# Moving a four-byte constant ahead of the identity, and 32 bytes of padding with it

## The chip, the cores and the metric

The kernel runs on one core of one Trainium2 chip. The metric is the device time of one execution in microseconds. Before the change it is 815.84 us, the median of three runs (815.72 to 816.29).

## The reference, cut to what matters

One layer of a hybrid decoder trunk over 512 tokens and 1024 channels, in float32.

```python
u = rmsnorm(h, norm1_g)
a_glu, q, k, v, r, g_low, gate_a, gate_b = split_cols(u @ w_in)
c = a_glu[..., :1024] * sigmoid(a_glu[..., 1024:])
c = silu(layernorm(causal_dwconv(c, width=31)))          # conv branch
y_conv = c @ w_conv_out
o = gla_chunked(q, k, v, log_sigmoid(g_low @ w_gate_up + b_gate) / 16)   # 4 heads
y_gla = (rmsnorm(o) * silu(r)) @ w_gla_out
h = h + (sigmoid(gate_a) * y_conv + sigmoid(gate_b) * y_gla) @ w_o
z = causal_dwconv(rmsnorm(h, norm2_g) @ w_ffn_up, width=3)
h = h + (silu(z[..., :2816]) * z[..., 2816:]) @ w_ffn_down
out = rmsnorm(h, final_g)
```

The layer norm of the conv branch needs `1 / sqrt(var + EPS)`. The constant of this case is the `EPS` that the square root takes as its bias.

## The kernel before, in words

Nearly all of the work is matrix products. Each float32 operand is split into a high part that TensorE's one-pass float32 format (F32R) holds exactly and a low remainder, and a product is made of three matmuls that add into one PSUM bank: `mm3`, lines 554 (moving high by stationary low, for a tile of output channels), 555 (low by high) and 556 (high by high). A weight block of 128 x 1024 arrives by DMA in a tile `raw`. ScalarE makes its high part `whi` (lines 435 and 468), VectorE its low part `wlo` (lines 437 and 477). Some products, on pairs or quads of tiles, are done in seven block products in place of eight; the sums that these need (`xq`, `usq`, `hq`, `gainq`, `btmpq`, `sumsq`, `sums`) are made by VectorE and GpSimd and split in the same way. Their matmuls are 256 columns wide where they go by tiles of output channels, the plain ones 512.

In a product by tiles of channels (`col_tile`) the activations move and the weights are stationary; in a product by tiles of tokens (`row_half` and the seven products of `w_r`, `w_o` and `w_down`) the weights move and the activations are stationary. The profile names the moving operand first: `mm<-uh,wlo` moves `uh` through `wlo`.

The order of the work is fixed when the program is built. `order` lists the weight blocks as they are used, `load`, `refill` and `split_weight` keep the loads and splits a few blocks ahead of TensorE, and `fill` places pieces of the conv taps and of the sums behind each weight split, by a share that the list gives each piece. The first stage is written out by hand (`manual_schedule`). Nothing of this order depends on where a tile lies in SBUF.

Where a tile lies is set by the order in which pools are opened and tiles are asked for. `const`, `weights`, `acts`, `temps`, `heap` and `conv` (later `ffn`) lie one behind the other from the low end of SBUF; `edge`, `gla`, `r`, `late`, `conv_hi` and `residual` are placed from the high end downwards. Every tile takes a multiple of 32 bytes of each partition: `eps`, four bytes, has byte 4448, and the next tile begins at 4480. The function `trunk_layer` opens the constant pool with a tile that nobody uses, `PADS[0]` bytes long (line 162); `PADS[1]` does the same for `edge`, `PADS[2]` for the middle of `temps` (line 852).

Byte addresses within a partition in the built program of before; the last column is what the argument uses.

| tiles | pool | first byte | byte modulo 256 |
|---|---|---|---|
| `ident` | const | 1568 | 32 |
| `pp` | const | 2080 | 32 |
| `ones`, `mhalf` | const | 3904, 4416 | 64 |
| `eps` | const | 4448 | 96 |
| `shares`, `run64`, `keep` | const | 4480, 4992, 6016 | 128 |
| `gains` | const | 6144 | 0 |
| `raw`, `whi`, `wlo` | weights | from 6176 on | 32 |
| `uh`, `ul`, `sums` | acts | from 55328 on | 32 |
| `x`, `un`, `xq`, `oa`, `gainq`, some `kept` | temps | from 88096 on | 32 |
| `tmp`, `btmp`, `btmpq` | temps | from 107680 on | 160 |
| `h`, `hq`, and `yh`, `sh`, `ah` and their low parts | heap, ffn | from 124704 on | 32 |
| `c`, `usq` | conv, ffn | from 177952 on | 32 |
| `ch` | conv_hi | from 199680 on | 0 |
| `sumsq` | late | from 216064 on | 0 |
| `hres` | residual | from 211968 on | 0 |
| `gate_up`, `att`, `q`, `k`, `state` | gla | from 200704 on | 0 |

A matmul reads pieces of these tiles that begin a multiple of 512 bytes further on, so their bytes have the same remainder. `ch` and `c` are the high and the low part of the conv branch's normalized channels (line 1063): `ch` lies at the high end, `c` at the low end.

`eps` is written once, by GpSimd at line 649, and read once, by ScalarE's square root at line 1044.

Of the kernel before, what the change touches and what calls it, by code (L numbers as in the profile page):

```python
# [10 lines left out]
F32 = mybir.dt.float32  # L11
# [7 lines left out]
P = 128  # L19
# [35 lines left out]
WARM = (6, 1)  # L55
MID = 4
EARLY = 2
PADS = (416, 992, 768)
ET = mybir.EngineType
SEVEN = {"w_o": KT // 2, "w_down": FT // 2, "w_r": KT // 2}  # L60

# [40 lines left out]
def trunk_layer(ctx: ExitStack, tc: tile.TileContext, a: dict, out: bass.AP):  # L102
    nc = tc.nc

    def pool(name, bufs, space=None):
        kw = {"space": space} if space is not None else {}
        return ctx.enter_context(tc.tile_pool(name=name, bufs=bufs, **kw))
# [7 lines left out]
    cp = pool("const", 1)  # L115
# [13 lines left out]
    def nm(s):  # L129
        return f"{s}_{next(names)}"  # L130
# [30 lines left out]
    for i, part in enumerate((cp, edge)):  # L161
        part.tile([P, PADS[i] // 4], F32, name=nm("pad"))


    ident = cp.tile([P, P], F32, name="ident")
    make_identity(nc, ident)
    pp = cp.tile([P, PP_N], F32, name="pp")
    gate_up = gp.tile([P, HEADS * DK], F32R, name="gate_up")
    ones = cp.tile([P, P], F32, name="ones")
    mhalf = cp.tile([P, NT], F32, name="mhalf")  # L170
    eps = cp.tile([P, 1], F32, name="eps")
    shares = cp.tile([P, P], F32R, name="shares")
    run64 = cp.tile([P, T], BF16, name="run64")
    keep = cp.tile([P, P], U8, name="keep")
# [2 lines left out]
    def load_consts():  # L177
        tc.keep_in_program_order(nc.sync.dma_start(pp, a["pp"]))
        nc.gpsimd.memset(shares.bitcast(F32), -1.0 / D)
        nc.gpsimd.memset(run64, 1.0)  # L180
        nc.gpsimd.memset(run64[:, 0:T:64], 0.0)

        kf = tmp(P)
        nc.gpsimd.memset(kf, 1.0)
        nc.gpsimd.affine_select(
            kf, kf, pattern=[[1, P]], compare_op=ALU.is_ge, fill=0.0, base=0, channel_multiplier=-1
        )
        nc.gpsimd.tensor_copy(keep, kf)
        nc.gpsimd.memset(att, 0.0)
# [661 lines left out]
    start.__exit__(None, None, None)  # L851
    tp.tile([P, PADS[2] // 4], F32, name=nm("pad"))
    load_consts()
# [1205 lines left out]
```

## Time and profile before

| | us |
|---|---|
| median of three runs | 815.84 |
| the profiled execution | 815.9 |
| its span, first to last instruction | 814.2 |
| TensorE (PE) busy in it | 806.4 |
| VectorE (DVE) busy | 708.0 |
| ScalarE (ACT) busy | 494.9 |
| GpSimd (POOL) busy | 188.5 |

The profiled execution takes 1.7 us more than its span and stands 0.06 us from the median. The granted TensorE clock is 0.999 of full. A matmul's own duration overlaps the next one's, so the distance between the starts of two matmuls is what a matmul costs; both are used below.

### The profile page before, as it was taken

To read this page: it belongs to the slowest core of one execution; us is meant where nothing else is said; L and a number is where in the kernel's file an instruction comes from. 1 tells how busy PE (TensorE), PEld (TensorE's weight loads), DVE (VectorE), ACT (ScalarE), POOL (GpSimd) and SP (SyncE) were. 2 spreads that over 40 slices of the span, in tenths; PEclk is the share of its full clock that TensorE was granted. 3 is DMA by queue.
4 is the path that set the end of the run, shared out by engine and by line. 5 is a ranking of instruction groups with operands and counts; after the bars stand their busy time and mean duration, and the time that the engine had idled before them with its cause. 6 is when DMAs were issued, how large, how long until landed. Compare 5 with 4: busy or idle time off the path is not lost.

```text
span 814.2 us, 11423 instructions
## 1 busy us (share of the span) xinstructions
PE 806.4 (99%) x4185; PEld 689.9 (85%) x4185; DVE 708.0 (87%) x1120; ACT 494.9 (61%) x761; POOL 188.5 (23%) x166
## 2 busy tenths in 40 slices
PE   9999999999999999999999999999999999999997
PEld 7888888788888798989888898898889988899885
DVE  6779999998998898786679899979966999789996
ACT  6667788677556785593434655556445563466655
POOL 2025433332204222022001100320133310612010
PEclk9999999999999999999999999999999999999999
DMA  9488858745832443432458513146632446334662
GB/s 334 150 195 174 197 159 173 164 114 129 197 85 83 148 125 104 146 113 96 164 126 205 187 60 122 52 155 156 148 128 87 141 118 167 106 104 158 178 130 105
DMA packets 41385, 115.71 MB, mean 142 GB/s; under 512 B 7960, under 2 KB 13216, under 8 KB 41328
## 3 DMA queue, kind: packets, MB, share of 16 engines
q1 hardware_dynamic: 33968, 89.01, 32.0%
q0 software_dynamic: 7200, 25.69, 18.2%
q8 instruction: 33, 0.54, 0.3%
q14 instruction: 24, 0.20, 0.1%
q10 hardware_dynamic: 160, 0.27, 0.1%
HBM read 110.76 MB, written 3.15 MB: 140 GB/s over the span
## 4 chain that ended last, share of the span: by engine, by line
PE 84%; DVE 14%; issue 1%; ACT 1%; DVEq 0%; ACTq 0%
PE mm L554 20%; PE mm L555 20%; PE mm L556 20%; DVE c L916 5%; PE cv L555 4%; PE cv L554 4%; PE cv L556 4%; DVE aside L916 3%; PE ax L556 2%; PE ax L555 2%; PE ax L554 2%; PE mm L772 1%; PE ax L1232 1%; PE ax L1234 1%; DVE wlo L437 1%
## 5 line engine op out<-in xcount | busy, mean ns | idle before, releaser
L554 PE MATMUL mm<-uh,wlo 128*128 128x512 f32 (+1 forms) x532 | 193.8, 364 | 0.3 <-DVE wlo L477 0.3
L555 PE MATMUL mm<-ul,whi 128*128 128x512 f32 (+1 forms) x532 | 191.6, 360 | 0.0
L556 PE MATMUL mm<-uh,whi 128*128 128x512 f32 (+1 forms) x532 | 191.5, 360 | 0.0
L437 DVE TENSOR_TENSOR wlo<-raw,whi 128x1024 fp32r<-128x1024 f32 x82 | 97.8, 1198 | 29.6 <-ACT whi L435 25.9
L405 POOL TENSOR_TENSOR raw<-raw,raw 128x512 f32<-128x512 f32 x39 | 60.6, 1554 | 241.0 <-DVE wlo L437 134.3
L554 PEld LDWEIGHTS mm<-uh,wlo 128*128 128x128 f32 x532 | 100.5, 189 | 15.8 <-DVE wlo L477 0.7
L556 PEld LDWEIGHTS mm<-uh,whi 128*128 128x128 f32 x532 | 100.4, 189 | 15.4
L555 PEld LDWEIGHTS mm<-ul,whi 128*128 128x128 f32 x532 | 100.5, 189 | 14.7
L435 ACT CAST whi<-raw 128x1024 fp32r<-128x1024 f32 x82 | 78.9, 965 | 36.9 <-PE mm L556 15.1
L468 ACT CAST whi<-raw 128x1024 fp32r<-128x1024 f32 x80 | 83.5, 1047 | 27.5 <-PE mm L556 13.1
L477 DVE TENSOR_TENSOR wlo<-raw,whi 128x1024 fp32r<-128x1024 f32 x50 | 64.7, 1299 | 7.2 <-ACT whi L468 7.1
L435 ACT CAST whi<-kept 128x1024 fp32r<-128x1024 f32 (+1 forms) x40 | 40.1, 1008 | 33.7 <-DVE kept L381 17.5
L437 DVE TENSOR_TENSOR wlo<-kept,whi 128x1024 fp32r<-128x1024 f32 (+1 forms) x40 | 48.3, 1211 | 5.5 <-ACT whi L435 5.4
L916 DVE SCALAR_TENSOR_TENSOR aside<-cv,pp,aside 128x255 f32<-128x255 f32 (+6 forms) x112 | 52.0, 465 | 0.0
L916 DVE SCALAR_TENSOR_TENSOR c<-aside,btmp,c 128x247 f32<-128x247 f32 (+13 forms) x93 | 52.0, 565 | 0.0
L916 DVE SCALAR_TENSOR_TENSOR c<-cv,pp,c 128x247 f32<-128x247 f32 (+13 forms) x93 | 43.1, 463 | 1.4 <-ACT c L912 1.4
L470 ACT ACTIVATE wlo<-raw 128x1024 fp32r<-128x1024 f32 x28 | 29.4, 1059 | 19.1 <-PE mm L554 19.1
L1770 DVE SCALAR_TENSOR_TENSOR tmp<-mm,pp,tmp 128x511 f32<-128x511 f32 (+1 forms) x42 | 31.2, 742 | 3.5 <-ACT tmp L1767 3.5
L1388 ACT COPY tmp<-mm 128x256 f32<-128x256 f32 x38 | 14.0, 368 | 30.3 <-PE mm L556 29.7
L1541 DVE TENSOR_TENSOR hres<-hres,mm 128x512 f32<-128x512 f32 (+1 forms) x37 | 24.6, 674 | 4.3 <-PE mm L556 2.5
L1770 DVE SCALAR_TENSOR_TENSOR tmp<-tmp,pp,tmp 128x511 f32<-128x511 f32 (+1 forms) x32 | 27.8, 888 | 0.4
L555 PE MATMUL cv<-ul,whi 128*128 128x512 f32 (+1 forms) x72 | 25.6, 356 | 0.0
(517 smaller groups left out, 2087.8 us busy)
## 6 DMA issues: line engine op xcount, KB each, us to landing
raw<-in_w_up_dram SPq DMA_DIRECT2D x44, 512.0 KB, 3.3
raw<-in_w_glu_dram SPq DMA_DIRECT2D x16, 512.0 KB, 4.9
raw<-in_w_down_dram SPq DMA_DIRECT2D x16, 512.0 KB, 4.5
wlo<-in_w_glu_dram POOLq DMA_DIRECT2D x12, 512.0 KB, 7.1
kept<-in_w_down_dram POOLq DMA_DIRECT2D x9, 512.0 KB, 5.3
raw<-in_w_v_dram SPq DMA_DIRECT2D x8, 512.0 KB, 6.4
raw<-in_w_qk_dram SPq DMA_DIRECT2D x8, 512.0 KB, 6.1
raw<-in_w_gb_dram SPq DMA_DIRECT2D x8, 512.0 KB, 4.4
```

What stands on the lines that cost most here:

```text
L405: work = nc.gpsimd.tensor_tensor(out, x, y, ALU.add)
L435: nc.scalar.copy(hi, raw)
L437: two_low[:] = [nc.vector.tensor_tensor(lo, raw, hi.bitcast(F32), ALU.subtract)]
L468: nc.scalar.copy(hi, raw)
L470: pace[0] = nc.scalar.mul(lo, raw, -1.0)
L477: pace[0] = nc.vector.tensor_tensor(lo, raw, hi.bitcast(F32), ALU.subtract)
L554: nc.tensor.matmul(acc, ll, rh, start=first, stop=False, **kw)
L555: nc.tensor.matmul(acc, lh, rl, start=False, stop=False, **kw)
L556: nc.tensor.matmul(acc, lh, rh, start=False, stop=last, **kw)
L916: nc.vector.scalar_tensor_tensor(out[:, j:], x[:, : half_t - j], w, out[:, j:], ALU.mult, ALU.add)
L1541: done = nc.vector.tensor_tensor(hres[t, n][:, c], hres[t, n][:, c], acc[:, c], op)
L1770: nc.vector.scalar_tensor_tensor(z[:, s:], acc[:, : T - s], w[j], z[:, s:], ALU.mult, ALU.add)
```

## The change

The tile `eps` is asked for before `ident` and not after `mhalf`, and the unused tile ahead of both shrinks by 32 bytes, from 416 to 384. No instruction is added, removed or written in another order.

```diff
-PADS = (416, 992, 768)
+PADS = (384, 992, 768)
...
+    eps = cp.tile([P, 1], F32, name="eps")
     ident = cp.tile([P, P], F32, name="ident")
     make_identity(nc, ident)
     pp = cp.tile([P, PP_N], F32, name="pp")
     gate_up = gp.tile([P, HEADS * DK], F32R, name="gate_up")
     ones = cp.tile([P, P], F32, name="ones")
     mhalf = cp.tile([P, NT], F32, name="mhalf")
-    eps = cp.tile([P, 1], F32, name="eps")
     shares = cp.tile([P, P], F32R, name="shares")
```

## The prediction

> **What bounds the kernel now.** I read the page's busy times first, then TensorE's waits, then the chain that ended last.
>
> ```profile
> span 814.2 us, 11423 instructions
> PE 806.4 (99%) x4185; PEld 689.9 (85%) x4185; DVE 708.0 (87%) x1120; ACT 494.9 (61%) x761; POOL 188.5 (23%) x166
> PE 84%; DVE 14%; issue 1%; ACT 1%; DVEq 0%; ACTq 0%
> PE mm L675 <- DVE ones L647: 1.1, 1, 1.1
> PE mm L554 <- DVE wlo L477: 0.3, 1, 0.3
> ```
>
> TensorE is busy for 806.4 of 814.2 us and waits by name for 1.4 us in all, never for a DMA. So the time is the sum of the distances between matmul starts, and a change that moves only addresses matters through that distance first. I therefore asked whether it already differs with where the operands lie. The chain shows two stages with the same work, 512-column matmuls in groups of three; each row is a start and a length in us.
>
> ```profile
> 500.54 0.23 PE cv L556
> 501.22 0.23 PE cv L556
> 501.90 0.23 PE cv L556
> ...
> 404.87 0.23 PE mm L556
> 405.57 0.23 PE mm L556
> ...
> 425.87 0.23 PE mm L556
> ```
>
> In the first stage a group of three takes 0.68 us (501.22 - 500.54). In the second, 30 groups take 425.87 - 404.87 = 21.00 us, 0.70 each. The clock is granted in full in both. The second is the product by `w_conv`, with `ch` moving. The durations, by operands (line, operation, count: minimum/median/maximum ns, or busy us, mean ns):
>
> ```profile
> L554 PE MATMUL mm<-uh,wlo 128*128 128x512 f32 x384 | 151.8, 395 | 0.3 <-DVE wlo L477 0.3
> L555 PE MATMUL mm<-ul,whi 128*128 128x512 f32 x384 | 149.7, 390 | 0.0
> L556 PE MATMUL mm<-uh,whi 128*128 128x512 f32 x384 | 149.6, 390 | 0.0
> L556 PE MATMUL mm<-whi,yh 128*128 128x512 f32 x30 | 11.7, 389 | 0.0
> L554 PE MATMUL mm<-ch,wlo x48: 397/397/400, 364.8 to 425.9; 128*128 128x512 f32 x48
> L556 PE MATMUL mm<-ch,whi x48: 390/397/397, 365.2 to 426.4; 128*128 128x512 f32 x48
> L555 PE MATMUL mm<-c,whi 128*128 128x512 f32 x48 | 18.9, 393 | 0.0
> L554 PE MATMUL cv<-ch,wlo x16: 392/396/400, 376.1 to 403.5; 128*128 128x512 f32 x16
> L556 PE MATMUL mm<-whi,sumsq x12: 389/396/397, 268.5 to 279.0; 128*128 128x512 f32 x12
> L555 PE MATMUL mm<-wlo,sumsq x12: 393/396/397, 268.2 to 278.7; 128*128 128x512 f32 x12
> L554 PE MATMUL mm<-whi,sumsq x8: 393/395/397, 268.0 to 272.9; 128*128 128x512 f32 x8
> L555 PE MATMUL cv<-wlo,sumsq x4: 394/397/397, 273.8 to 275.9; 128*128 128x512 f32 x4
> ```
>
> Where both operands have remainder 32 modulo 256 (`uh`, `ul`, `yh`, `whi`, `wlo`), an undisturbed matmul has 389. Where one has 0 and the other 32, it has 395 to 397, whether the odd one moves (`ch`) or is stationary (`sumsq`). `c` has remainder 32 itself, but alternates with `ch`, and has 393. 397 + 393 + 397 against three times 389 is 20 ns, which is the 0.70 against 0.68 of the chain. Two more rows say whether it is the remainder itself or the difference between the two operands that counts. These are 256 columns wide.
>
> ```profile
> L556 PE MATMUL ax<-gainq,whi x32: 283/283/283, 536.6 to 751.9; 128*128 128x256 f32 x32
> L556 PE MATMUL mm<-btmpq,whi x28: 276/280/284, 554.9 to 750.4; 128*128 128x256 f32 x28
> L555 PE MATMUL cv<-sumsq,whi x12: 277/279/285, 294.0 to 343.8; 128*128 128x256 f32 x12
> L554 PE MATMUL mm<-sumsq,wlo x28: 280/282/364, 292.4 to 396.9; 128*128 128x256 f32 x28
> ```
>
> `gainq` (difference 0) sits at exactly 283, every time. `btmpq` has remainder 160, a difference of 128; `sumsq` 0, a difference of -32. Both scatter in the same band around 280, though one starts on a multiple of 64 bytes and the other doesn't. I read this as a fixed rhythm that matmul and weight load fall into when their bytes agree modulo 256, and that they miss otherwise: at 512 columns the rhythm is the faster state, at 256 the slower by 1 to 4 ns. An equal shift of both operands leaves it.
>
> The Trainium skill ("TensorE: Matmul & The Clock Gate", section Step-by-step) says that TensorE has two independent SBUF read ports, so that loading the next weights takes no read bandwidth from the running matmul. By that rule the operands' relative place can't matter, and the terms below would all be nothing. The 397 against 389 speaks against it here.
>
> **The change part by part.** The unused tile loses 32 bytes and `eps` takes them, so `ident`, `pp`, `ones` and `mhalf` stay. `shares` and all that follows from the low end begin 32 bytes lower. The high end stays. Remainders 32 become 0, 160 becomes 128, `shares` 96. No instruction, wait, DMA or queue position is added or moved: the write of `eps` and its one reader stay where they are in their queues.
>
> 1. *Pairs that both move* (nearly all matmuls): same difference, same rhythm, 0. No row shows a one-pass pair with 0 and 0. Its bounds are the odd rows: 8 ns more for 512 columns (397 against 389), 7 ns less for 256 columns (276 against 283). I take 0, by the evidence of `btmpq` and `sumsq`.
>
> 2. *`ch` by weights* changes to difference 0. There are 64 + 64 matmuls with `ch` (two forms of 48 and two of 16) and 64 with `c`, so 64 groups at 20 ns: -1.28 us. Some comes back, because the rhythm takes a few matmuls to find after a change of width:
>
> ```profile
> L554 PE MATMUL mm<-uh,wlo 128*128 128x512 f32 x4 | 1.6, 394 | 0.0
> L555 PE MATMUL mm<-ul,whi 128*128 128x512 f32 x3 | 1.2, 393 | 0.0
> ```
>
> These are the first ones after narrow matmuls, between 530 and 538 us: 4 x 5 + 3 x 4 = 32 ns for one start. The `ch` matmuls stand between narrow ones for their first half; I count some eight starts, 0.25 us, an estimate. Net -1.0, between 0 and -1.3.
>
> 3. *`sumsq` stationary*: 12 + 12 + 8 + 4 = 36 matmuls at 7 ns, -0.25. They end in the one stage in which the chain leaves TensorE for ScalarE and VectorE, and a part of it may be waited away: -0.15, between 0 and -0.25.
>
> 4. *`sumsq` moving*, 256 columns: it finds the slower rhythm. The rows give 1 ns (282 to 283) for the larger forms and 4 for the smaller, about 100 matmuls: +0.2, between 0 and +0.4.
>
> 5. *Other engines.* A copy and a subtraction of 128 x 512 with tiles at remainder 0, and with none:
>
> ```profile
> L1063 ACT CAST ch<-btmp x8: 602/614/622, 348.3 to 363.8; 128x512 fp32r<-128x512 f32 x8
> L1351 ACT CAST btmpq<-xq x2: 619/620/620, 480.0 to 482.1; 128x512 fp32r<-128x512 f32 x2
> L1064 DVE TENSOR_TENSOR c<-btmp,ch x8: 677/683/1774, 349.0 to 364.4; 128x512 fp32r<-128x512 f32 x8
> L1356 DVE TENSOR_TENSOR usq<-xq,btmpq x2: 684/684/685, 496.6 to 500.6; 128x512 fp32r<-128x512 f32 x2
> out_dram<-tmp SPq DMA_DIRECT2D x2, 256.0 KB, 2.6
> out_dram<-hres SPq DMA_DIRECT2D x2, 256.0 KB, 2.7
> ```
>
> 614 against 620 and 683 against 684 ns; a store from remainder 160 lands in 2.6 us, from 0 in 2.7. I take 0 for all of it. What hides a difference of a few per cent is that TensorE waits for them for 0.3 us; if that cover went, 1% of VectorE's 708 us would be 7 us.
>
> Sum: -1.0 - 0.15 + 0.2 = -0.95 us. The profiled execution is 815.9 us (814.2 of span and 1.7 around it), which becomes 814.95; the median of the runs shown, 815.84, becomes 814.9.
>
> **The rivals.** *The places don't matter* (the skill's two ports): then `ch` is slow for a reason of its own, such as lying at the high end, and the time stays at 815.84. For it: no row shows `ch` by weights with difference 0. Against it: `sumsq` as stationary operand shows the same 7 ns in another product at another time.
>
> *A start on a multiple of 256 is itself faster*, so that a matmul spares a piece of its reading. Price by the scattered rows, 7 ns (276 against 283): on the 3 x 384 matmuls with `uh` and `ul` alone -8 us, 807.8; with the others up to twice that. Against it: `sumsq` starts on such a multiple and is no faster than `btmpq`. The skill's page on TensorE (section Back-to-back issue gap) gives 512 / 2.4 + 2.5 = 216 ns as the distance for 512 columns; the chain's 0.68 / 3 is 227, so by that page there are 11 ns to win, some 13 us on these 1,152 matmuls.
>
> *Remainder 0 is itself slower*, for the moving operand as for the stationary one. The rows with `ch` and `sumsq` fit this too, since every slow one has a 0 in it. It decides at the first `uh` matmul: 389 becomes 397, and 3 x 384 x 8 ns is +9.2 us, 825.0, with the other wide groups up to 832. Against it: `btmpq` has no 0 in it and loses the rhythm all the same.
>
> *A VectorE instruction falls behind GpSimd's.* In the stage near 285 us one subtraction on the chain lasts nearly twice its mean:
>
> ```profile
> 285.59 2.23 DVE wlo L437
> L437 DVE TENSOR_TENSOR wlo<-raw,whi 128x1024 fp32r<-128x1024 f32 x82 | 97.8, 1198 | 29.6 <-ACT whi L435 25.9
> ```
>
> Shifted by 0.2 us, a second one could do so: +1.0 us, which with the sum gives 815.9.
>
> **How the numbers follow.** Forecast 0.60, no effect of places 0.12, faster starts 0.15, slower starts 0.08, the VectorE collision 0.05. About 0.2% (1.6 us) is what a measurement of this kernel can tell from no change; that is 814.2 below and 817.5 above. The forecast's bounds on terms 2 to 4 run from -1.55 to +0.4, and a little more where the rhythm is found more often than now; I give 0.18 of its 0.60 to more than 1.6 us. Faster: 0.15 + 0.18 = 0.33. Slower: 0.08 + 0.03 from a collision of two = 0.11, and 0.01 for what I have not seen. Same: 0.55. The range holds the forecast, no effect and the collision, with the small end of the faster starts: 812.2 to 816.8. It leaves out the large ends on both sides, some 0.2.
>
> **What would show it.** Right: the medians of `mm<-ch,wlo` and `mm<-ch,whi` go to 389, the groups in the `w_conv` stage stand 0.68 us apart, `sumsq` moving shows 283, and `uh` by `wlo` stays at 389 and 283. `ch` still at 397 means that the places don't matter. `uh` at 397, or below 385, means that the remainder itself counts, and makes the prediction wrong, as would a new wait of TensorE of over 2 us.

## The result and the profile after

The changed kernel takes 814.39 us, the median of 21 runs (813.86 to 815.13), against 815.84 us for the kernel before (815.32 to 816.29, 21 runs). The ratio is 0.9983, with a 95% interval of 0.9977 to 0.9989: 1.45 us less, and by the interval between 0.9 and 1.9 us. The forecast was 814.9 us, 0.95 us less. The larger part of the chance, 0.55, went to a change of less than 1.6 us either way, and that is how it came out, though a change of zero lies outside the interval.

The page and TensorE's waits after the change:

```profile
span 813.4 us, 11423 instructions
PE 805.4 (99%) x4185; PEld 690.3 (85%) x4185; DVE 707.8 (87%) x1120; ACT 494.8 (61%) x761; POOL 191.7 (24%) x166
PE mm L675 <- DVE ones L647: 1.1, 1, 1.1
PE cv L554 <- DVE r L1598: 0.3, 1, 0.3
PE cv L555 <- DVE wlo L437: 0.2, 1, 0.2
PE mm L779 <- DMA raw<-in_w_v_dram: 0.2, 1, 0.2
```

The instructions are the same, in the same order on every engine; TensorE's share of the span is the same and its named waits, 1.8 us in all, stay far below 1% of it. What changed is how long a few of its matmuls take. Groups of matmuls and single operands after the change, in the two forms used before (busy us, mean ns; or minimum/median/maximum ns):

```profile
L554 PE MATMUL mm<-uh,wlo 128*128 128x512 f32 x384 | 152.0, 396 | 0.0
L555 PE MATMUL mm<-ul,whi 128*128 128x512 f32 x384 | 149.8, 390 | 0.0
L556 PE MATMUL mm<-uh,whi 128*128 128x512 f32 x384 | 149.7, 390 | 0.0
L554 PE MATMUL mm<-ch,wlo x48: 388/390/397, 365.0 to 425.3; 128*128 128x512 f32 x48
L556 PE MATMUL mm<-ch,whi x48: 388/389/390, 365.5 to 425.8; 128*128 128x512 f32 x48
L555 PE MATMUL mm<-c,whi 128*128 128x512 f32 x48 | 18.7, 390 | 0.0
L556 PE MATMUL mm<-whi,sumsq x12: 388/389/390, 268.7 to 278.9; 128*128 128x512 f32 x12
...
L555 PE MATMUL mm<-wlo,sumsq x12: 389/389/390, 268.5 to 278.7; 128*128 128x512 f32 x12
L555 PE MATMUL cv<-sumsq,whi x12: 282/283/284, 294.1 to 344.1; 128*128 128x256 f32 x12
L556 PE MATMUL ax<-gainq,whi x32: 283/283/284, 535.9 to 751.1; 128*128 128x256 f32 x32
L556 PE MATMUL mm<-btmpq,whi x28: 276/280/285, 554.1 to 749.7; 128*128 128x256 f32 x28
```

`ch` went from 397 to 389 and 390, `c` between them from 393 to 390, `sumsq` as stationary operand from 396 to 389. `sumsq` as moving operand of 256 columns went up from 279 to 283. `uh` and `ul`, whose start and whose weights' start moved together, stayed within 1 ns, and `btmpq`, 128 bytes off its weights before and after, stayed at 280. In the `w_conv` stage the chain now has the distance of the undisturbed stages, 407.56 - 406.88 = 0.68 us for three:

```profile
406.88 0.23 PE mm L556
...
407.56 0.23 PE mm L556
```

Six points of the trace bound five stages; 6.2 to 6.3 us follow the start of the last matmul. The table has the distance between the starts of the first or last matmuls with the operand named, in us, from one profile of each kernel (the third is the changed kernel profiled again with the last experiments):

| from | to | before | after | again |
|---|---|---|---|---|
| start | first `sumsq` | 268.01 | 268.30 | 267.60 |
| first `sumsq` | first `oa` | 27.65 | 27.53 | 27.51 |
| first `oa` | first `ch` | 69.10 | 69.19 | 69.20 |
| first `ch` | last `ch` | 61.65 | 60.74 | 60.74 |
| last `ch` | last matmul | 381.49 | 381.43 | 381.51 |

The `ch` stage is 0.91 us shorter in both, the stage with `sumsq` stationary 0.12 to 0.14, and the stage from `oa` on, in which `sumsq` moves, 0.1 longer. From the first `sumsq` to the end of the span it is 546.18 us before, 545.12 after and 545.19 again. The first stage differs by 0.7 us between two profiles of one and the same kernel, and most of that (0.5 us) is there before 36 us.

### The profile page after: what moved, and what is told of

It reads as the page before. It is cut to its first block, busy times and chain, and to the rows that moved or that the text cites. A ratio compares the mean times of both kernels' runs of the same rounds, so it can differ in the third digit from the quotient of the medians.

```text
span 813.4 us, 11423 instructions
## 1 busy us (share of the span) xinstructions
PE 805.4 (99%) x4185; PEld 690.3 (85%) x4185; DVE 707.8 (87%) x1120; ACT 494.8 (61%) x761; POOL 191.7 (24%) x166
## 4 chain that ended last, share of the span: by engine, by line
PE 77%; DVE 14%; issue 5%; ACT 1%; DMA 1%; POOL 1%; SPq 0%; DVEq 0%; ACTq 0%; POOLq 0%
PE mm L554 18%; PE mm L555 18%; PE mm L556 18%; DVE c L916 5%; PE cv L555 4%; PE cv L556 4%; PE cv L554 4%; DVE aside L916 3%; PE ax L556 2%; PE ax L555 2%; PE ax L554 2%; PE mm L772 2%; DVE wlo L437 2%; DMA raw<-in_w_v_dram 1%; PE cv L772 1%
## 5 line engine op out<-in xcount | busy, mean ns | idle before, releaser
L555 PE MATMUL mm<-ul,whi 128*128 128x512 f32 (+1 forms) x532 | 191.7, 360 | 0.0
L405 POOL TENSOR_TENSOR raw<-raw,raw 128x512 f32<-128x512 f32 x39 | 63.7, 1633 | 239.4 <-DVE wlo L437 121.4
```

The source lines that it names most:

```text
L405: work = nc.gpsimd.tensor_tensor(out, x, y, ALU.add)
L555: nc.tensor.matmul(acc, lh, rl, start=False, stop=False, **kw)
```

## The experiments

**Is it the difference, or the start itself?** The kernel before, with the high end moved up instead of the low end down:

```diff
-PADS = (416, 992, 768)
+PADS = (416, 960, 768)
```

> The kernel before, with one change: the unused tile at the high end is 960 bytes, not 992, so that everything placed from the high end lies 32 bytes higher. ch, sumsq, hres, att have remainder 32 modulo 256, as uh and the weights have had all along: the difference between the two operands of a matmul is 0, but no start is a multiple of 256. Theory (the difference counts): the same gain as the change, some 1.4 us, 814.4 us; mm<-ch,wlo and mm<-ch,whi at 389 to 390 ns, sumsq moving at 283. Rival (a start on a multiple of 256, or of 64, is what counts): nothing of the gain, since every start now misses such a multiple: 815.8 us or more, ch at 396.

Measured: 815.02 us against 815.70 for the kernel before on the same chip, ratio 0.9993 (0.9984 to 1.0002). The time alone doesn't settle it, since its interval takes in no change and most of the change's gain. The rows do. The first two are `ch`, the third `sumsq`, the last one of TensorE's waits:

```profile
L554 PE MATMUL mm<-ch,wlo x48: 389/389/396, 364.1 to 424.3; 128*128 128x512 f32 x48
L556 PE MATMUL mm<-ch,whi x48: 389/389/389, 364.5 to 424.8; 128*128 128x512 f32 x48
L555 PE MATMUL cv<-sumsq,whi x12: 283/283/283, 293.2 to 343.1; 128*128 128x256 f32 x12
PE cv L554 <- DVE r L1598: 0.4, 1, 0.4
```

None of these operands starts on a multiple of 256, and `ch` has its 389 all the same; its stage takes 60.74 us, as after the change. For these rows the start itself is not what counts. The time, though, missed the forecast of 814.4 us by 0.6, and the kernel with the low end moved down by 32 bytes, on the same chip in the next experiment, had 814.43. Some of that can be seen. The matmuls with `sumsq` stationary are at 389 here too, but their stage takes 27.63 us: the next matmul waits for VectorE, and the distance to it from the last of them grew from 0.54 us to 0.80, after the change only to 0.69. From the first `sumsq` to the end it is 545.35 us, 0.8 less than before, where the change had 1.1. What else the low end gives is not shown.

**The shift without moving `eps`.**

```diff
-PADS = (416, 992, 768)
+PADS = (384, 992, 768)
```

> The kernel before, with the unused tile at 384 bytes and eps left behind mhalf: the shift of 32 bytes alone. ident, pp, ones and mhalf move with the rest here. Theory: all of the change's gain comes from the shift, so 814.4 us, and where eps and the identity lie is worth nothing. Rival: the constants' own place counts (eps and ident), then it stays away from 814.4 by 0.5 us or more.

Measured: 814.43 us, ratio 0.9986 (0.9977 to 0.9994), 1.27 us less than the kernel before. All of the gain that can be told is the 32 bytes; where `eps` and the identity lie is worth nothing that can be told.

**The dose: all weights off by 32 bytes.** A pad ahead of the weights and one behind them, so that only `raw`, `whi` and `wlo` move:

```diff
         part.tile([P, PADS[i] // 4], F32, name=nm("pad"))
+    wp.tile([P, 8], F32, name=nm("pad"))
+    up.tile([P, 56], F32, name=nm("pad"))
```

> The changed kernel with raw, whi and wlo 32 bytes higher (a pad of 32 bytes ahead of them, one of 224 behind), so that every matmul of the split products has a difference of 32 between its operands. Theory: some 2,590 matmuls of 512 columns lose 6 to 7 ns each and some 1,250 of 256 columns win about 2: +16 to +18 us less 2.5, about 828 us; mm<-uh,wlo goes from 389 to 395 to 397 wherever undisturbed. Rival (the high end of SBUF is slow for ch): uh stays at 389 and the time at 814.4 us.

Measured: 826.12 us, ratio 1.0128 (1.0114 to 1.0142), 11.7 us over the changed kernel's 814.4. The two added lines move the lines of `mm3` from 554 to 556 on, here and in some runs below.

```profile
span 824.6 us, 11423 instructions
...
L556 PE MATMUL mm<-uh,wlo 128*128 128x512 f32 x384 | 153.6, 400 | 0.0
L557 PE MATMUL mm<-ul,whi 128*128 128x512 f32 x384 | 151.8, 395 | 0.0
L558 PE MATMUL mm<-uh,whi 128*128 128x512 f32 x384 | 151.9, 396 | 0.0
L556 PE MATMUL mm<-uh,wlo 128*128 128x256 f32 x148 | 41.8, 282 | 0.0
```

`uh` and `ul` lie where the changed kernel has them, and lose 4 to 6 ns each because their weights moved. So `ch` isn't slow for lying at the high end. The expected 828 us was 2 us too high: the mean loss in these groups is 5 ns, not 6 to 7, because part of these matmuls were out of the rhythm before (the group means were 396 and 390, not 389). 2,590 x 5 ns less 1,250 x 1.5 ns is 11.1 us, an estimate. The `ch` stage, again with a difference of 32, went back to 61.60 us.

**A map of places.** 32 matmuls to a group, with the moving operand's start set off by a number of bytes:

```python
acc = ps.tile([P, T], F32, tag="mm", name=name, bufs=4)
for i in range(count):
    s = dw // size + P * (i % 8)
    o = d // size + (n * (i % 2) if n < T else 0)
    nc.tensor.matmul(acc[:, :n], ww[:, s : s + P], mm[:, o : o + n], start=i == 0, stop=i == count - 1)
```

> Nothing of the layer: a row of matmuls, 32 to a group, that take weights of 128 columns from one F32R tile and move 512 (wide) or 256 (half) columns of another. The group's name has the byte by which the moving operand's start differs from the weights' start modulo 256 (d0 to d240 in steps of 16), or the byte by which both are shifted (both16, both32, both64, both128); three groups in bfloat16 (bf). Theory: wide has its shortest distance, 227 ns, at d0 and at all four of both, and 233 at d32 and d224 (that is, -32); half has 120 at d0 and about 118 elsewhere. Rival (absolute start counts): both32 differs from d0. Open, without a forecast: how wide the good place is (16, 32, 64 bytes), and if some difference is better than 0.

Groups of the map (busy us of the group, mean ns of one):

```profile
L39 PE MATMUL wide_d0x<-m,w 128*128 128x512 f32 x32 | 7.4, 390 | 0.0
L39 PE MATMUL wide_both16x<-m,w 128*128 128x512 f32 x32 | 7.5, 392 | 0.0
L39 PE MATMUL wide_both64x<-m,w 128*128 128x512 f32 x32 | 7.4, 390 | 0.0
L39 PE MATMUL wide_d32x<-m,w 128*128 128x512 f32 x32 | 7.6, 396 | 0.0
L39 PE MATMUL wide_d224x<-m,w 128*128 128x512 f32 x32 | 7.6, 396 | 0.0
L39 PE MATMUL half_d0x<-m,w 128*128 128x256 f32 x32 | 4.0, 283 | 0.0
L39 PE MATMUL half_d64x<-m,w 128*128 128x256 f32 x32 | 3.8, 276 | 0.0
L39 PE MATMUL bf_d0x<-mb,wb 128*128 128x512 bf16 x32 | 7.1, 380 | 0.0
L39 PE MATMUL bf_d32x<-mb,wb 128*128 128x512 bf16 x32 | 7.1, 379 | 0.0
```

The mean distance from one start to the next, in ns, worked out from the starts in each group without its first eight:

| difference, bytes | 0 | 32 | 64 | 96 | 128 | 160 | 192 | 224 |
|---|---|---|---|---|---|---|---|---|
| 512 columns | 226.7 | 233.3 | 228.9 | 233.4 | 233.1 | 234.3 | 233.2 | 233.4 |
| 256 columns | 120.0 | 116.7 | 113.3 | 119.8 | 118.6 | 117.3 | 113.3 | 118.4 |

Of the steps of 32 bytes that tiles can take, 0 alone has the 226.7 at 512 columns. Both operands shifted by 32, 64 or 128 have it too (226.7 to 227.1). Shifted by 16, both together, they don't: 229.9 ns, against the forecast. So the difference alone is not the whole rule: an equal shift kept the rhythm at the multiples of 32 that were tried, which is all that a tile's place can be, and not at 16. The 256 columns are slowest at 0, with 96 hardly faster. The bfloat16 groups have 216 ns at all three of their places (0, 32 and 128); only F32R showed a dependence.

**A finer map, and narrower weights.** The same loop with steps of 4 bytes, and weights of 64 and 32 columns:

> Nothing of the layer: the same row of matmuls as the first map of places, 24 to a group, with the difference in steps of 4 bytes from 0 to 80 and from 224 to 252, and, in groups with w64 and w32 in the name, weights of 64 and 32 columns at differences of 0, 32 and 64 bytes. Theory (the load of the next weights meets the moving operand's reading): with narrower weights the slow places go, and 512 columns come down towards the 216 ns that bfloat16 had at every place; at full weights the good place around 0 and 240 is 16 to 20 bytes wide. Rival (the moving operand's own reading is slow at those places): the narrower weights change nothing at a difference of 32, 233 ns.

| difference, bytes | 0 | 4 | 12 | 20 | 28 | 60 | 64 | 236 | 240 | 244 | 252 |
|---|---|---|---|---|---|---|---|---|---|---|---|
| 512 columns | 226.7 | 236.6 | 228.9 | 240.0 | 226.7 | 226.7 | 228.9 | 226.7 | 226.7 | 240.0 | 226.7 |
| 256 columns | 120.0 | 123.4 | 116.7 | 123.5 | 118.3 | 116.7 | 117.8 | 116.6 | 117.5 | 122.9 | 120.0 |

There is no single good place 16 to 20 bytes wide: good and bad ones alternate every few bytes. At 64 bytes and 256 columns the two maps disagree, 113.3 against 117.8 ns, so the difference alone doesn't fix the rhythm; what ran just before was another group. The narrower weights went against the theory; the rival's forecast, no change at a difference of 32, nearly held (233.5 ns with 128 columns, 231.0 with 64, 232.2 with 32), but it had no place for a change at 0:

```profile
L39 PE MATMUL wide_w32d0x<-m,w 128*32 128x512 f32 x24 | 5.7, 394 | 0.0
L39 PE MATMUL wide_w32d32x<-m,w 128*32 128x512 f32 x24 | 5.7, 394 | 0.0
L39 PE MATMUL half_w32d0x<-m,w 128*32 128x256 f32 x24 | 2.9, 276 | 0.0
```

With 32 columns of weights the 512-column distance is 231.6 and 232.2 ns at differences of 0 and 32, and never comes near 216. That the next weights' load collides with the moving operand's reading is thus not shown. The width of the weights does change the distance at a difference of 0 (from 226.7 to 231.6, and from 120.0 to 113.3 at 256 columns), but a narrower product also has fewer rows of output, so this doesn't show that it is the load. What the rhythm is made of stays open.

**A better layout, first try.** Only tiles that move 256 columns at a time are laid off the weights by 64 bytes:

```diff
-PADS = (384, 992, 768)
+PADS = (384, 992, 640)
...
+    tp.tile([P, 16], F32, name=nm("pad"))
+    hp.tile([P, 16], F32, name=nm("pad"), bufs=1)
...
+    fp.tile([P, 16], F32, name=nm("pad"))
...
+            if not padded:
+                padded.append(fp.tile([P, 16], F32, name=nm("pad")))
...
+            late_pad.append(late.tile([P, 16], F32, name=nm("pad")))
...
+            chp.tile([P, 48], F32, name=nm("pad"), bufs=1)
```

> The changed kernel, with the tiles that move only 256 columns at a time laid 64 bytes off the weights (xq, gainq, btmpq, usq at a remainder of 64, sumsq at 192), by pads of 64 bytes and of 192; all others keep a remainder of 0. The map of places gives 113.3 ns at 64 and 192 for 256 columns, against 120 at 0 and 118 at 128; for 512 columns 229 at 64 against 227. Theory: 224 matmuls with xq and gainq, 96 with usq and 100 with sumsq win 6.7 ns, 64 with btmpq 4.7: -3.1 us; 96 with oa, which shares xq's slots, and 36 with sumsq stationary lose about 2: +0.3. Less 0.3 for hq, which stays at 0 between sumsq's matmuls: -2.5 us against the changed kernel, some 811.9 us, a ratio of 0.995. Rival (in the real order, in which the same weights are loaded twice, the places of the map don't hold): 814.4 us.

Measured: 814.55 us, ratio 0.9988 (0.9979 to 0.9997) to the kernel before, so nothing that can be told from the changed kernel.

```profile
L558 PE MATMUL ax<-xq,whi x32: 279/279/279, 530.1 to 745.0; 128*128 128x256 f32 x32
L557 PE MATMUL ax<-usq,whi x32: 279/279/279, 530.0 to 744.9; 128*128 128x256 f32 x32
L556 PE MATMUL mm<-oa,wlo x28: 388/394/481, 294.7 to 352.4; 128*128 128x512 f32 x28
L556 PE MATMUL mm<-whi,sumsq x8: 392/392/392, 267.2 to 272.0; 128*128 128x512 f32 x8
```

The 276 of the first map didn't come: `xq` and `usq` have a duration of 279, the value of the second map, in place of 283. What a matmul costs, the distance between starts, fell by less: `xq` by `whi` from 119.9 to 118.2 ns, not to 113.3. The last stage is 0.37 us shorter than after the change (381.06 against 381.43) and the `ch` stage, in which `sumsq` moves too, 0.15; the stage from `oa` on is 0.41 longer (69.60 against 69.19), mainly since `oa` went from 389 to 394. `sumsq` as stationary operand has 392 against 389. So what was won was given back.

**A better layout, second try.** By the finer map, a difference of 60 bytes costs nothing at 512 columns and wins 3 ns at 256. The activations of the up-projection move both widths, so their tiles get 256 spare bytes and they begin 15 elements in:

```diff
+    def act_tile(name, at=0):
+        t = up.tile([P, 4 * T + 64], F32R, tag="u", name=nm(name), bufs=4)
+        return t[:, at : at + 4 * T].rearrange("p (k t) -> p k t", k=4)
...
-            u2.extend(new_acts())
+            u2.extend(new_acts(15))
```

> The changed kernel itself, on the chip of the next two, to compare them with it: some 1.3 us below the kernel before, 814.3 us.

> The changed kernel with the second set of activations (uh and ul of the up-projection) 60 bytes further on in their tiles, so that 600 matmuls of 512 and 432 of 256 columns have a difference of 60 between moving operand and weights. The finer map gives 226.7 ns at 60 for 512 columns, as at 0, and 116.7 for 256, against 120 at 0. Theory (the map holds in the real order): uh by wlo at 512 columns stays at 389, at 256 goes from 283 to 279 or 280; 432 x 3.3 ns = -1.4 us, 812.9 us. Rival (which rhythm a stream falls into depends on more than the difference, as the two maps disagree at 64: 113.3 and 117.8): the 512-column matmuls lose the rhythm too, up to 600 x 6.7 ns = +4 us.

> The same, and xq, gainq, btmpq and usq with a remainder of 64, sumsq left at 0. Those four showed 279 to 280 ns at 64 in the run before, against 283, and 281 for btmpq: 320 x 3.5 and 64 x 1 ns = -1.2 us; 84 to 96 matmuls with oa showed 388 to 394 against 389: +0.3. Theory: -0.9 us more than with the activations alone, 812.0 us. Rival: what is won in TensorE is waited away elsewhere; then TensorE's waits grow.

Measured on one chip, against 815.66 us for the kernel before:

| kernel | us | ratio to before | 95% interval |
|---|---|---|---|
| the changed kernel | 814.27 | 0.9984 | 0.9975 to 0.9993 |
| activations 60 bytes off | 813.53 | 0.9973 | 0.9963 to 0.9983 |
| and four 256-column tiles 64 bytes off | 812.87 | 0.9965 | 0.9951 to 0.9979 |

The groups from 430 us on, after the change and with the activations 60 bytes off:

```profile
L556 PE MATMUL mm<-uh,whi 128*128 128x512 f32 x152 | 59.2, 389 | 0.0
L556 PE MATMUL mm<-uh,whi 128*128 128x256 f32 x88 | 24.9, 283 | 0.0
```

```profile
L556 PE MATMUL mm<-uh,whi 128*128 128x512 f32 x152 | 59.1, 389 | 0.0
L556 PE MATMUL mm<-uh,whi 128*128 128x256 f32 x88 | 24.4, 278 | 0.0
```

And with the four tiles as well, TensorE's longest wait and one of these tiles:

```profile
L557 PE MATMUL ax<-usq,whi 128*128 128x256 f32 x32 | 8.9, 278 | 0.0
...
PE mm L675 <- DVE ones L647: 1.1, 1, 1.1
```

The time fell by 0.74 us from the first row to the second, where 1.4 was forecast; the medians' intervals are too wide to tell the two apart. Durations would say 432 x 5 ns = 2 us, but they are not the cost. The stage in which these matmuls lie, from the last `ch` to the last matmul, says 1.14: 381.51 us in the changed kernel, 380.37 with the activations 60 bytes off. The profiled spans differ by 812.8 - 811.0 = 1.8 us, of which 0.65 is the first stage, which varies by that much. With the four tiles as well the last stage falls to 379.40, another 0.97, but the stage from `oa` on goes from 69.18 to 69.76, so 0.58 of it is lost again, twice what was forecast for `oa`. The third kernel is 2.8 us faster than the kernel before and 1.4 faster than the changed one; its interval and the changed kernel's overlap, but it is the lowest of all in the medians, and TensorE's longest wait stayed 1.1 us.

## Why the prediction was right

*What bounds the kernel.* That the change comes through the distance between matmul starts held from the first `sumsq` on. TensorE's named waits were 1.4 us before and 1.8 us after, of which 1.1 is the same one. Copies, subtractions and stores at the new places gave nothing that could be seen, as term 5 had it (the copy to `ch` 614 ns before and 618 after, the subtraction 683 and 682); GpSimd's busy time rose from 188.5 to 191.7 us, but no wait of TensorE names it.

*The reading of `btmpq` and `sumsq`* was the step that carried the argument, and the experiment with the high end moved up bore it out: the difference of the two operands counts and not the start. It was right in this kernel for a reason narrower than the text made it. "Their bytes agree modulo 256" is the one good place for 512 columns among the multiples of 32, which are all that a tile can take; between them lie others (28, 60, 236, 240, 252). And "an equal shift of both operands leaves it" fails for a shift of 16 (229.9 ns); the change's shift was 32.

*Term 1*, pairs that move together, was taken as 0 between bounds of +8 and -7 ns. It measured 0 to 1 ns in the three largest groups. The other terms can be summed over the distances from these matmuls' starts to the next ones. *Term 2*, `ch` and `c`, was -1.0 and measured -0.99 us (44.74 to 43.74). *Term 3*, `sumsq` stationary, was -0.15 and measured -0.12: without the last one the matmuls won 0.27 us, and the wait behind the last one grew by 0.15, as the term had it. (The term counts 36 of 40 such matmuls, and the stage is not the one place where the chain leaves TensorE: the prediction's own row has 14% of the chain on VectorE.) *Term 4*, `sumsq` moving, was +0.2 and measured +0.15 (11.91 to 12.06). Together that is -0.95 forecast and -0.96 measured.

The medians say -1.45, with an interval that begins at -0.9. From the first `sumsq` to the end the profiles lost 1.06 us, so if the median is taken as it stands, some 0.4 us was won ahead of it, where the prediction has no term. Moving the high end instead won 0.68 in the median and 0.8 from the first `sumsq` on, which leaves nothing for that first stage. Both differences are near the noise, and one profile of each kernel can't show such a gain where profiles differ by 0.7. What it is stays open, and so the forecast of the time is borne out only at the edge of the interval. The text's own limit, that 1.6 us is what can be told from no change, was too wide: the interval is 0.5 us to either side.

*The rivals.* That the places don't matter fell with `ch` at 389. That a start on a multiple of 256 is faster, or slower, in itself fell with `uh` at 389 and 283 on such a start, and with the same `ch` at 389 on a start that isn't one. The rule that the Trainium skill gives for the two read ports ("TensorE: Matmul & The Clock Gate", section Step-by-step) doesn't cover F32R here: 389 against 397 with nothing moved but one operand, and 11.7 us when the weights moved. The 216 ns that the Trainium skill gives for 512 columns ("TensorE: Matmul & The Clock Gate", section Back-to-back issue gap, there the gap of an isolated matmul) agrees with the bfloat16 groups, 216; no F32R group of the maps came below 226.7. The collision on VectorE didn't show: near 285 us one subtraction is long, 2.3 us, as before. The price of slower starts at all wide groups, "up to 832", was too low: some 2,360 wide matmuls without `ch`, `c` and `sumsq` at 8 ns are 19 us, 835, an estimate.

*The expectations that failed.* The first better layout was to win 2.5 us and won none: the forecast took 113.3 ns from one group of one map, for a place where the next map had 117.8. The high end moved up was to have all of the gain and had half of it. A shift of 16 bytes was to keep the rhythm and didn't, and narrower weights were to come down towards 216 ns and didn't.

## What to carry to other kernels

Where TensorE sets the time and its rows of one shape fall into two narrow bands of duration, where the operands start is worth a look: here 32 bytes of padding too many at one end of SBUF cost some 1.4 us, about 1 us of it seen in matmul rows, and 32 bytes between all weights and all activations cost 11.7. The place of the constant itself was worth nothing. A new small constant belongs where it moves no large tile against another, or gets its padding back. A place is to be tried in the kernel itself, since a map of single places held for some of them and not for others, and its worth is to be read from the distances between starts, not from durations, which fell by 4 ns where the distance fell by under 2.

## What the runs showed that was not expected

At 256 columns the rhythm that is best at 512 is among the slow ones: 120.0 ns at a difference of 0 against 113.3 to 119.8 at other multiples of 32, so one layout can't serve both widths at such a place, while 60 bytes did (226.7 and 116.7). F32R matmuls of 512 columns took 226.7 ns at best, bfloat16 ones 216 at each place tried. And narrower weights made wide F32R matmuls slower at a difference of 0, 231.6 ns with 32 columns against 226.7 with 128.
